# Who asks for the first eight expert blocks: ScalarE in one burst, or SP one by one between the query weights

## The chip, the cores and the metric

The kernel runs on one core of one Trainium2 chip. The metric is the device time of one execution in microseconds (us); the time of a kernel is the median of its runs.

## What is computed

Two transformer blocks on 256 tokens of width 1024. The change sits in the second half of the first block, a product-key expert layer:

```python
q = (h @ w_pq).reshape(B, S, PEER_HEADS, 2, PEER_DHALF)          # 8 heads, 2 halves of 128
sc = jnp.einsum("bshcd,hcnd->bshcn", q, sub_keys)                # 128 keys for each half
s_top, i_top = lax.top_k(sc, PEER_TOPK)                          # 16 of each half
cand = s_top[..., 0, :, None] + s_top[..., 1, None, :]
best, pos = lax.top_k(cand, PEER_TOPK)                           # 16 experts per head
gate = jax.nn.softmax(best, axis=-1)
a = jax.nn.gelu(jnp.einsum("ced,cd->ce", u_emb[idx], hx), approximate=False)
out = jnp.einsum("ce,ced->cd", g * a, v_emb[idx])                # 16384 experts in u_emb, v_emb
```

All else (convolution and window attention before it, a second block of attention and feed-forward layers behind it) is the same in both kernels.

## The kernel before, in words

All dense weights lie in one array `wst` of 279 tiles of 128x1024 floats (512 KB), used in order. `load_tile` (L140) asks for a tile on SP's queue into one of four buffers `raw`; `split_tile` makes `whi` of it on ScalarE (L150) and the rest `wlo` on VectorE (L157) or, for the tiles listed in `POOL`, in four pieces on GpSimd (L155), with three buffers of each. `mm_t` (L168) multiplies a 128x128 block three times on TensorE: `whi` with the upper half of the activations (L176), `whi` with the lower (L177), `wlo` with the upper (L178).

The **query stage** is the loop at L968 in `peer`: 16 chunks, one for each head and half, which use the tiles 66 to 81. Here a chunk goes by its number 0 to 15. Each is 24 products (L176 to L178); ScalarE copies its result to `pq` (L972), and two chunks later `scores` (L954) multiplies `pq` with the keys (L957) and ScalarE scales that to `sc` (L959). VectorE finds the 16 largest of each row (`top16`, L869 to L878) and GpSimd widens their indices (`tops`, L896). `wlo` is made by GpSimd for all chunks but 4 and 10, for these by VectorE. Work that belongs to no chunk is put in by `pump`: at chunk 3 `normalise` (L945), eight VectorE operations that write `hn` (L947). They need `rb`, the scale of each token, which comes down a chain over four engines at the head of the stage: sums of squares on TensorE (L319), their inverse root on VectorE (L363 to L369, `rr`), two diagonals `dg` on ScalarE (L380), one product on TensorE (L382), a copy on ScalarE (L383).

At the head of the stage GpSimd's queue also stores the residual, 1 MB (`park`, L847).

Behind the query stage comes the **U sweep**: 128 blocks of 128 experts, each a 512 KB tile of `ut` and eight products (`ublock`, L1050, products at L1054). The first eight blocks lie in the eight buffers `row` (`first`, L865), which lie where tensors of the stage before lay; the others go through ten buffers that were `raw`, `whi` and `wlo` (`whole`, L1038). The sweep is dense for 160 tokens. For the other 96 the rows of the chosen experts are gathered by GpSimd's queue into the same buffers `row` (L1648), which starts once the indices are known: `pick` (product L1638 on TensorE, then L1640 to L1644 on VectorE). The **V sweep** (L1168 to L1190) does the same with `vv`. From the U sweep on the order on each engine is that of the code (`in_order`).

In the query stage a scheduler sets the order on each engine from the order of the code and its own estimates, so an edit at one place can move instructions on other engines. Each engine then takes its instructions strictly in turn, and a wait holds back all that stands behind it; an engine that asks for a DMA spends its turn on it. Of the semaphores in the rows below, `DMAHW0` to `DMAHW7` count transfers asked for by SP and ScalarE, taken in turn, `DMASW` those of GpSimd, and the rest are named for the engine waited for.

Of the kernel before, what the change touches and what calls it, by code (L numbers as in the profile page):

```python
# [93 lines left out]
N = ROWS[-1][0]  # L94

RB = 8


class Kernel:
# [742 lines left out]
    def peer(self):  # L842
        nc, a = self.nc, self.a
# [19 lines left out]

        pr = self.open("rows", side="right")
        first = [pr.tile([128, D], F32, name="row", bufs=RB) for _ in range(RB)]  # L865
        for i, raw in enumerate(first):
            nc.scalar.dma_start(raw, a["ut"][i])

        def top16(v, idx, src, work):  # L869
            nc.vector.max(v[:, :8], src)  # L870
# [74 lines left out]
        def normalise():  # L945
            for cc in range(C):
                nc.vector.scalar_tensor_tensor(hn[:, cc], x[:, cc], self.p("norm2_g", cc), rb, op0=ALU.mult, op1=ALU.mult)  # L947
                yield 0.4
# [5 lines left out]
        def scores(h, c, qt):  # L954
            for tt in (1, 0):
                sp = self.pp.tile([128, 128], F32, name="ax", bufs=4)
                nc.tensor.matmul(sp, qt[:, tt * 128:(tt + 1) * 128], sk[:, 2 * h + c], start=True, stop=True)  # L957
                sc = p2t.tile([128, 128], F32, name="sc", bufs=32)
                nc.scalar.activation(sc, sp, AF.Copy, scale=r[:, tt:tt + 1])  # L959
                scs[tt, h, c] = sc  # L960

            if c == 1:
                u0, u1 = (unit(tt, h, [scs[tt, h, i] for i in range(2)]) for tt in range(2))
                firsts.append(u1)
                self.bg.insert(next((k for k, u in enumerate(self.bg) if k and u not in firsts), len(self.bg)), u1)
                self.bg.append(u0)

        for h in range(8):  # L968
            for c in range(2):
                pt = self.chunk(xs)  # L970
                qt = p2q.tile([128, T], F32, name="pq", bufs=4)
                nc.scalar.activation(qt, pt, AF.Copy)  # L972
                self.later(2, lambda h=h, c=c, qt=qt: scores(h, c, qt))
                if h * 2 + c == 3:
                    self.bg.insert(0, normalise())
                self.pump(QP, True)
        self.flush()

# [59 lines left out]
        def whole(src, n, eng=nc.sync):  # L1038

            name = ring[n % len(ring)]  # L1040
            raw = self.sp.tile([128, 1024], F32, name=name, bufs=ring.count(name))
            eng.dma_start(raw, src)
            return raw
# [6 lines left out]
        def ublock(i, n_t):  # L1050
            raw = first[i] if i < RB else whole(a["ut"][i], i - RB)
            pt = self.pp.tile([128, N], F32, name="mm", bufs=4)
            for k in range(C):
                nc.tensor.matmul(pt, raw[:, k * 128:(k + 1) * 128], hn[:, k, :N], start=(k == 0), stop=(k == C - 1))  # L1054
            self.tick()
            if n_t == 0:
                nc.scalar.activation(G(i), pt, AF.Gelu)
            else:
                ac = pg.tile([128, N], F32, name="ac", bufs=3)
                nc.scalar.activation(ac[:, :n_t], pt[:, :n_t], AF.Gelu)  # L1060
                if n_t < N:
                    nc.scalar.activation(G(i, slice(n_t, N)), pt[:, n_t:], AF.Gelu)
                muls.append((G(i, slice(0, n_t)), ac[:, :n_t]))
# [50 lines left out]
        i = 0  # L1114
# [49 lines left out]
        for q in range(4):  # L1164
            for k in range(4):
                nc.tensor.matmul(acc[q].rearrange("p a b -> p (a b)")[:, k * 128:(k + 1) * 128], zero, zero, start=True, stop=False, skip_group_check=True)
        nv = 128 - RB
        for i in range(64, 128):  # L1168
# [433 lines left out]
class RowGroup:  # L1602
# [19 lines left out]
    def activations(self):  # L1622

        nc, k = self.k.nc, self.k
        x = self.pool.tile([128, D], F32, name="row", bufs=RB)
        nc.scalar.activation(x.rearrange("p (c k t) -> p c k t", c=C, t=self.n),
# [19 lines left out]
    def row(self, table, s):  # L1646
        t = self.pool.tile([128, D], F32, name="row", bufs=RB)
        self.k.nc.gpsimd.indirect_dma_start(t, None, table, bass.IndirectOffsetOnAxis(ap=self.idx[:, s:s + 1], axis=0))  # L1648
        return t
# [20 lines left out]
def fetched(groups):  # L1670
# [4 lines left out]
    begun = []  # L1675
    for g, f, s in todo + [(None, 0, 0)] * (RB - 1):
        if g is not None:
# [193 lines left out]
```

## Time and profile before

| | us |
|---|---|
| runs | 1575.03, 1572.44, 1576.2 |
| median | 1575.03 |
| profiled execution | 1572.59 |
| its span, first to last instruction | 1570.7 |
| TensorE busy in the span | 1520.5 (97%) |
| VectorE busy | 1111.3 (71%) |
| ScalarE busy | 647.5 (41%) |
| GpSimd busy | 546.5 (35%) |

The span lies 1.9 us below the profiled execution's own time, and that 2.4 us below the median of the runs. PE stands for TensorE, PEld for its weight loads, DVE for VectorE, ACT for ScalarE, POOL for GpSimd, SP for SyncE; a q behind a name means its sequencer, which issues DMAs. TensorE is busy nearly all the time, so what can be won lies in the few stretches where it is not, or where its granted clock is below 1.

### The profile page before, as it was taken

What the parts mean: (1) busy time and instruction counts of PE and PEld (TensorE: products, weight loads), DVE (VectorE), ACT (ScalarE), POOL (GpSimd) and SP (SyncE); (2) the same over time, 40 slices, a digit from 0 to 9 for tenths busy, and PEclk for the clock granted to TensorE, in tenths of its full rate; (3) what the DMA queues carried; (4) which work ended last, traced back from release to release, by engine and by line L of the source; (5) the groups of instructions that cost most, each with busy time, mean ns of one, the idle gap of its engine ahead of it and who ended that gap; (6) DMA issues with size and microseconds to landing.
All of it is one profiled execution on the core that took longest, in us unless ns stands there. A gap on an engine that the chain in (4) does not pass through costs nothing.

```text
span 1570.7 us, 30113 instructions
## 1 busy us (share of the span) xinstructions
PE 1520.5 (97%) x11514; PEld 1462.8 (93%) x11514; DVE 1111.3 (71%) x2510; ACT 647.5 (41%) x1398; POOL 546.5 (35%) x593
## 2 busy tenths in 40 slices
PE   9999988999999998999899999999999999999997
PEld 8988987999999998999899999889999997899986
DVE  6989876979998998544344449777776558776655
ACT  4588454422355542000000034565544446655543
POOL 4957804704587776655455301000000030000000
PEclk9999999999999999999999999999999999999999
DMA  6534547449999999999999955626656586365563
GB/s 201 172 116 128 169 144 277 149 160 366 409 408 408 408 408 405 396 409 409 410 409 408 408 181 184 215 94 197 193 183 187 180 204 190 124 196 177 177 191 115
DMA packets 109680, 399.18 MB, mean 254 GB/s; under 512 B 12516, under 2 KB 12931, under 8 KB 109024
## 3 DMA queue, kind: packets, MB, share of 16 engines
q1 hardware_dynamic: 72720, 262.18, 48.2%
q0 software_dynamic: 35232, 130.64, 21.8%
q10 hardware_dynamic: 1584, 4.45, 0.8%
q8 instruction: 90, 1.47, 0.4%
q14 instruction: 54, 0.44, 0.1%
HBM read 395.04 MB, written 6.11 MB: 255 GB/s over the span
## 4 chain that ended last, share of the span: by engine, by line
PE 81%; DMA 10%; DVE 4%; issue 2%; POOL 1%; ACT 1%; ACTq 0%; POOLq 0%; DVEq 0%
PE mm L1054 17%; PE mm L176 14%; PE mm L178 13%; PE mm L177 13%; PE ax L1162 12%; DMA row<-vv,idx 3%; DMA whi<-vv 2%; DMA raw<-wst 2%; PE mm L244 2%; PE mm L243 2%; PE mm L242 2%; POOL wlo L155 1%; PE ax L1092 1%; DMA wlo<-vv 1%; DVE wlo L157 1%
## 5 line engine op out<-in xcount | busy, mean ns | idle before, releaser
L150 ACT ACTIVATE whi<-raw 128x1024 fp32r<-128x1024 f32 x275 | 290.5, 1059 | 604.4 <-PE ax L1162 281.9
L157 DVE TENSOR_TENSOR wlo<-raw,whi 128x1024 fp32r<-128x1024 f32 x213 | 262.5, 1235 | 115.0 <-ACT whi L150 110.9
L178 PE MATMUL mm<-xgh,wlo 128*128 128x256 f32 x1064 | 302.5, 284 | 3.7 <-DVE wlo L157 3.7
L176 PE MATMUL mm<-xgh,whi 128*128 128x256 f32 x1064 | 305.6, 287 | 0.0
L177 PE MATMUL mm<-xgl,whi 128*128 128x256 f32 x1064 | 302.1, 284 | 0.0
L1663 DVE SCALAR_TENSOR_TENSOR acc<-row,w,acc 128x1024 f32<-128x1024 f32 x94 | 120.8, 1285 | 153.1 <-DMA row<-vv,idx 152.8
L178 PEld LDWEIGHTS mm<-xgh,wlo 128*128 128x128 f32 x1064 | 204.9, 193 | 4.3 <-DVE wlo L157 3.9
L155 POOL TENSOR_TENSOR wlo<-raw,whi 128x256 fp32r<-128x256 f32 x248 | 180.4, 762 | 80.7 <-ACT whi L150 80.4
L176 PEld LDWEIGHTS mm<-xgh,whi 128*128 128x128 f32 x1064 | 204.8, 193 | 2.2 <-issue 1.5
L177 PEld LDWEIGHTS mm<-xgl,whi 128*128 128x128 f32 x1064 | 204.9, 193 | 0.2
L1648 POOL DMA_INDIRECT row<-vv,idx x96 | 127.0, 1323 | 99.7 <-DMA row<-vv,idx 71.0
L1162 PE MATMUL ax<-G,raw 128*128 128x160 f32 x816 | 122.2, 303 | 7.1 <-DMA raw<-vv 7.1
L1648 POOL DMA_INDIRECT row<-un,idx x96 | 110.6, 1153 | 38.6 <-DVE a L1653 18.3
L1162 PEld LDWEIGHTS ax<-G,raw 128*128 128x128 f32 x816 | 115.4, 193 | 7.4 <-DMA raw<-vv 7.4
L1653 DVE CUSTOM_DVE_ANT_0 junk<-row,h 128x1024 f32<-128x1024 f32 x96 | 120.0, 1250 | 0.4
L1054 PE MATMUL mm<-hn,raw 128*128 128x160 f32 x768 | 112.6, 300 | 0.0
L1054 PEld LDWEIGHTS mm<-hn,raw 128*128 128x128 f32 x768 | 106.3, 190 | 0.0
L177 PE MATMUL mm<-hl,whi 128*128 128x256 f32 x368 | 104.3, 283 | 0.0
L1162 PE MATMUL ax<-G,whi 128*128 128x160 f32 x624 | 95.9, 304 | 6.8 <-DMA whi<-vv 6.7
L630 DVE SCALAR_TENSOR_TENSOR ax<-u,cw,ax 128x256 f32<-128x256 f32 x227 | 99.3, 483 | 1.6 <-ACT ax L628 0.8
L1162 PEld LDWEIGHTS ax<-G,whi 128*128 128x128 f32 x624 | 89.6, 194 | 7.5 <-DMA whi<-vv 7.5
L1162 PE MATMUL ax<-G,wlo 128*128 128x160 f32 x608 | 90.8, 301 | 2.5 <-DMA wlo<-vv 2.5
(437 smaller groups left out, 3302.7 us busy)
## 6 DMA issues: line engine op xcount, KB each, us to landing
raw<-wst SPq DMA_DIRECT2D x278, 512.0 KB, 3.7
raw<-ut SPq DMA_DIRECT2D x48, 512.0 KB, 15.7
raw<-vv SPq DMA_DIRECT2D x38, 512.0 KB, 7.9
whi<-ut SPq DMA_DIRECT2D x36, 512.0 KB, 16.0
wlo<-ut SPq DMA_DIRECT2D x36, 512.0 KB, 15.7
whi<-vv SPq DMA_DIRECT2D x33, 512.0 KB, 7.8
wlo<-vv SPq DMA_DIRECT2D x26, 512.0 KB, 7.9
raw<-vv POOLq DMA_DIRECT2D x13, 512.0 KB, 17.0
```

The lines of the kernel that those rows point to most:

```text
L150: nc.scalar.activation(hi, raw, AF.Copy)
L155: nc.gpsimd.tensor_sub(lo[:, p], raw[:, p], hi[:, p])
L157: self.pin = nc.vector.tensor_sub(lo, raw, hi)
L176: nc.tensor.matmul(pt, w[:, s], xs[0][:, k], start=first, stop=False)
L177: nc.tensor.matmul(pt, w[:, s], xs[1][:, k], start=False, stop=False)
L178: nc.tensor.matmul(pt, lo[:, s], xs[0][:, k], start=False, stop=last)
L630: nc.vector.scalar_tensor_tensor(y[:, c] if k == 30 else ps, u[:, c, k:k + T], cw[:, c, k:k + 1], ps, op0=ALU.mult, op1=ALU.add)
L1054: nc.tensor.matmul(pt, raw[:, k * 128:(k + 1) * 128], hn[:, k, :N], start=(k == 0), stop=(k == C - 1))
L1162: nc.tensor.matmul(acc[d // 2][:, d % 2, :N], raw[:, d * 128:(d + 1) * 128], G(i), start=False, stop=False, skip_group_check=True)
L1648: self.k.nc.gpsimd.indirect_dma_start(t, None, table, bass.IndirectOffsetOnAxis(ap=self.idx[:, s:s + 1], axis=0))
L1653: self.k.nc.vector.tensor_tensor_reduce(junk, row, self.h, 1.0, 0.0, ALU.mult, ALU.add, self.a[:, s:s + 1])
L1663: self.k.nc.vector.scalar_tensor_tensor(self.acc, row, w, self.acc, op0=ALU.mult, op1=ALU.add)
```

## The change

The eight loads of `first` leave the head of the stage, where ScalarE asked for all of them (L866, L867), and are asked for by SP inside the loop: block k in the pass of chunk k + 3, so those of blocks 0 to 7 stand in the passes of chunks 3 to 10.

```diff
 RB = 8
+FB = 3
...
         first = [pr.tile([128, D], F32, name="row", bufs=RB) for _ in range(RB)]
-        for i, raw in enumerate(first):
-            nc.scalar.dma_start(raw, a["ut"][i])
...
                 if h * 2 + c == 3:
                     self.bg.insert(0, normalise())
+
+                if 0 <= h * 2 + c - FB < RB:
+                    nc.sync.dma_start(first[h * 2 + c - FB], a["ut"][h * 2 + c - FB])
                 self.pump(QP, True)
```

Behind the edit the line numbers of the changed kernel are higher by 1 (up to L865), lower by 1 (to L974) or higher by 2.

On SP's queue, around the query stage, `raw<-wst` are the weight tiles, `row<-ut` the eight expert blocks. Before, 81 weight tiles stood in a row ahead of the U sweep:

```order
L142 DMA raw<-wst 128x1024 x81
L1042 DMA raw<-ut 128x1024
L1042 DMA whi<-ut 128x1024
L1042 DMA wlo<-ut 128x1024
L1042 DMA raw<-ut 128x1024
```

and now, with what each waits for, from the weights of chunk 5 (first row) to those of chunk 10:

```order
L143 DMA raw<-wst 128x1024 [waits DMAHW1_49,Activation_49,Pool_49]
L977 DMA row<-ut 128x1024 [waits DMASW3_49,DMASW2_49,DMASW4_49,DMASW1_49,DVE_49]
L977 DMA row<-ut 128x1024
L977 DMA row<-ut 128x1024 [waits DMAHW2_49]
L143 DMA raw<-wst 128x1024 [waits DMAHW3_49,Activation_49,Pool_49]
L977 DMA row<-ut 128x1024 [waits DMAHW4_49]
L143 DMA raw<-wst 128x1024 [waits DMAHW5_49,Activation_49,Pool_49]
L977 DMA row<-ut 128x1024 [waits DMAHW6_49]
L143 DMA raw<-wst 128x1024 [waits DMAHW7_49,DVE_49]
L977 DMA row<-ut 128x1024 [waits DMAHW0_49]
L143 DMA raw<-wst 128x1024 [waits DMAHW1_49,Activation_49,Pool_49]
```

Three blocks now stand between the weights of chunks 5 and 6, then one behind the weights of each of the chunks 6 to 10.

On ScalarE at the head of the query stage, before:

```order
L867 DMA row<-ut 128x1024 [waits PE_49]
L867 DMA row<-ut 128x1024 x3
L867 DMA row<-ut 128x1024 [waits DMAHW3_49]
L867 DMA row<-ut 128x1024 [waits DMAHW4_49]
L867 DMA row<-ut 128x1024 [waits DMAHW5_49]
L867 DMA row<-ut 128x1024 [waits DMAHW6_49]
L972 ACTIVATE pq<-mm 128x256 [waits PE_49]
L380 ACTIVATE dg<-ident,rr 128x128 [waits DVE_49]
L380 ACTIVATE dg<-ident,rr 128x128
L972 ACTIVATE pq<-mm 128x256 [waits PE_49] x2
L150 ACTIVATE whi<-raw 128x1024 [waits Pool_49]
L383 ACTIVATE rb<-ax 128x256 [waits PE_49]
```

and now (`c_4400` and `c_4409` are two small tables for the gathered rows, which came later before):

```order
L1621 DMA c_4400<-cst 128x194
L1621 DMA c_4409<-cst 128x164
L151 ACTIVATE whi<-raw 128x1024
L971 ACTIVATE pq<-mm 128x256
L381 ACTIVATE dg<-ident,rr 128x128 x2
L971 ACTIVATE pq<-mm 128x256
L151 ACTIVATE whi<-raw 128x1024
L384 ACTIVATE rb<-ax 128x256
```

The eight loads are gone from ScalarE, and `whi` of chunk 3 stands ahead of the first `pq`. On TensorE the product with `dg` (L382, now L383) moved ahead by 19 products: it stood behind the last product of chunk 2 and stands now behind the fifth.

On VectorE at chunk 4, before:

```order
L947 SCALAR_TENSOR_TENSOR hn<-x,prm,rb 128x256 [waits Activation_49]
L947 SCALAR_TENSOR_TENSOR hn<-x,prm,rb 128x256 x7
L157 TENSOR_TENSOR wlo<-raw,whi 128x1024 [waits DMAHW4_49,PE_49,Activation_49]
L870 MAX tv<-sc 128x8 [waits Activation_49]
L872 MAX_INDEX iu<-tv,sc 128x8 [waits DVE_49]
```

and now:

```order
L158 TENSOR_TENSOR wlo<-raw,whi 128x1024 [waits DMAHW4_49,PE_49,Activation_49]
L946 SCALAR_TENSOR_TENSOR hn<-x,prm,rb 128x256 [waits Activation_49]
L946 SCALAR_TENSOR_TENSOR hn<-x,prm,rb 128x256 x7
L869 MAX tv<-sc 128x8 [waits Activation_49]
L871 MAX_INDEX iu<-tv,sc 128x8 [waits DVE_49]
```

`wlo` of chunk 4 now stands ahead of the eight `hn`. On GpSimd the first `tops` (L896, now L895), which needs the first `top16`, moved from behind `wlo` of chunk 6 to ahead of it.

## Rows read from the trace of the kernel before

**Rows 1.** The head of the page.

```profile
span 1570.7 us, 30113 instructions
```

**Rows 2.** Windows: stretch, its length, PE, PEld, DVE, ACT, POOL busy, PE clock, DMA share, GB/s.

```profile
260.00:265.00 5.00, 1.12 (x10) 0.91 (x8) 0.00 (x0) 0.35 (x2) 0.00 (x0) 1.00 1.01 414
265.00:270.00 5.00, 4.33 (x18) 3.73 (x19) 2.59 (x4) 4.79 (x11) 2.82 (x4) 0.66 1.03 419
270.00:275.00 5.00, 2.27 (x20) 2.06 (x18) 5.00 (x6) 1.85 (x4) 5.00 (x7) 1.00 0.62 214
275.00:280.00 5.00, 4.00 (x21) 4.00 (x22) 4.83 (x25) 0.00 (x0) 3.74 (x5) 0.66 0.78 233
```

**Rows 3.** The chain that ended last, in order of time: start, length, what.

```profile
253.58 10.07 DMA raw<-wst
...
268.11 6.17 DVE hn L947 x7
```

**Rows 4.** TensorE's timeline: start, length, line, operation [idle before <-releaser].

```profile
260.84 0.28 PE L178 MATMUL mm<-xgh,wlo 128*128 128x256 f32 x1
265.66 0.70 PE L382 MATMUL ax<-dg,ones 128*128 128x256 f32 x2 [4.54 <-ACT dg L380]
266.20 0.99 PE L957 MATMUL ax<-sk,pq 128*128 128x128 f32 x4
...
276.00 0.38 PE L178 MATMUL mm<-xgh,wlo 128*128 128x256 f32 x1 [3.73 <-DVE wlo L157]
...
280.24 0.61 PE L957 MATMUL ax<-sk,pq 128*128 128x128 f32 x4
...
283.51 0.61 PE L957 MATMUL ax<-sk,pq 128*128 128x128 f32 x4
```

**Rows 5.** ScalarE's timeline, and line L867 by itself (duration in ns: min/median/max).

```profile
252.63 0.34 ACTq L867 DMA_DIRECT2D row<-ut  x1
...
253.59 11.02 ACTq L867 DMA_DIRECT2D row<-ut  x6
264.65 0.38 ACT L972 ACTIVATE pq<-mm 128x256 f32<-128x256 f32 x1 [11.13 <-DMA raw<-wst]
...
L867 ACTq DMA_DIRECT2D row<-ut x8: 335/551/997, 252.6 to 264.1; - x8
```

**Rows 6.** Timelines of VectorE and GpSimd.

```profile
257.80 0.16 DVE L369 SCALAR_TENSOR_TENSOR rr<-ax,rr 128x2 f32<-128x2 f32 x1
267.41 6.88 DVE L947 SCALAR_TENSOR_TENSOR hn<-x,prm,rb 128x256 f32<-128x256 f32 x8 [9.45 <-ACT rb L383]
274.21 1.74 DVE L157 TENSOR_TENSOR wlo<-raw,whi 128x1024 fp32r<-128x1024 f32 x1
...
277.44 0.28 DVE L878 FIND_INDEX8 iu<-tv,scw 128x8 uint32<-128x128 f32 x1
...
254.07 2.80 POOL L155 TENSOR_TENSOR wlo<-raw,whi 128x256 fp32r<-128x256 f32 x4
```

**Rows 7.** An SP issue, DMA issues (KB, median us to landing), two windows as in rows 2.

```profile
256.90 0.33 SPq L142 DMA_DIRECT2D raw<-wst  x1
...
raw<-wst SPq DMA_DIRECT2D x278, 512.0 KB, 3.7
...
254.00:260.00 6.00, 6.00 (x54) 6.00 (x53) 2.33 (x12) 0.00 (x0) 2.85 (x5) 1.00 0.87 291
260.00:270.00 10.00, 5.44 (x28) 4.64 (x27) 2.59 (x4) 5.14 (x11) 2.82 (x4) 0.83 1.02 416
```

**Rows 8.** A wait within 245 to 320 us (total, times, longest); gathers; the pick; a window.

```profile
DVE tv L870 <- ACT sc L959: 3.0, 2, 1.7
...
L1648 POOL DMA_INDIRECT row<-un,idx x96: 943/976/1909, 357.3 to 614.9; - x96
...
352.53 0.29 DVE L1640 TENSOR_TENSOR own<-ax,c 128x128 f32<-128x128 f32 x1 [7.10 <-PE ax L1638]
...
360.00:900.00 540.00, 523.59 (x3984) 520.61 (x3983) 367.17 (x678) 111.09 (x410) 325.42 (x270) 0.99 1.02 406
```

## The prediction
> **What bounds the kernel now.** I read the page first, then windows over the query stage, then the chain of waits through the hole that they show, and last the timeline of each engine in it. The span is 1570.7 us [rows 1]. The query stage runs from about 252 to 318 us, and TensorE works through it without a break except in one place: of the 5 us from 260 it works 1.12, of those from 270 it works 2.27, and in the two slices between and behind them its granted clock is 0.66, a mixture of its two levels, 2.4 and 1.2 GHz, where it had been 1.00 [rows 2]. Each drop of the clock follows an idle stretch. The chain of waits leads through the same hole: a weight load that took 10.07 us and, behind ScalarE's late turn, seven of VectorE's `hn` [rows 3].
>
> How much does the hole cost? In the undisturbed part one chunk with its pair of score products takes 283.51 - 280.24 = 3.27 us, of which the scores are about 0.44 and the 24 products 2.83 [rows 4]. Between the last product of chunk 2, whose issue slot ends at 260.84 + 0.12 = 260.96, and the scores at 280.24 TensorE did the product with `dg` (266.20 - 265.66 = 0.54) and two such chunks (3, 4) with their scores: 0.54 + 2 x 3.27 = 7.08 us of work in 19.28 us. **The hole costs 12.2 us.** Its pieces: 4.7 idle up to 265.66, waiting for `dg` from ScalarE; 3.9 idle up to 276.00, waiting for `wlo` of chunk 4 from VectorE [rows 4]; the other 3.6 are the work done at the lower clock behind each.
>
> Why was ScalarE late? It asks for the first block at 252.63 and is then held in its own queue: the last six issues lie in one stretch of 11.02 us, and the copy `pq` behind them waited 11.13 us, in the end for a weight load [rows 5]. In the order, the fifth to eighth loads each wait on a DMA semaphore that a weight load of SP uses. So ScalarE stood still until a weight load had landed that itself had 2 MB of blocks and the 1 MB of `park` for company: 10.07 us [rows 3] where such a load normally takes 3.7 [rows 7]. Why was VectorE late? `rb` came late out of ScalarE, the eight `hn` took 6.88 us, and `wlo` of chunk 4 stood behind them [rows 6].
>
> **The change part by part.** *ScalarE loses eight issues and four waits.* By its new order it makes `whi` of chunk 3 as soon as chunk 0 has left its buffer (about 254.4 to 255.5), copies `pq` (255.9), and waits for `rr`, which VectorE ends at 257.96 [rows 6]; two `dg` follow by about 258.7. TensorE reaches the product with `dg` after five products of chunk 2, at about 258.05 + 5 x 0.12 = 258.65. With the passing on of the semaphore I charge a **new wait of 0.2 us**. The two small loads `c`, now ahead of `whi`, take less than the 0.9 us which ScalarE has before chunk 0 ends. From there TensorE finds every operand ready: chunk 2 ends at 261.6 with the `dg` product, scores and chunk 3 at 264.9, scores and chunk 4 at 268.2, the third scores at 268.6, where before they ended at 280.7. **The stage ends 12.2 - 0.2 = 12.0 us sooner.**
>
> *VectorE does `wlo` of chunk 4 ahead of `hn`.* `whi` of chunk 4 comes at about 260.2, `wlo` at 261.5 to 262.0 (1.23 us, or 1.74 as in rows 6), and TensorE wants it at 265.4. This move is needed: with `rb` at 260.5 and `hn` first, `wlo` would come at 260.5 + 6.88 + 1.74 = 269.1, and 3.7 us of idle time would stay.
>
> *What hides `hn` now.* VectorE ends it at 262.0 + 6.88 = 268.9 at the latest. The first `top16` ended 277.72 - 275.95 = 1.8 us behind the `wlo` [rows 6], so it ends by 270.7; GpSimd's first `tops` (0.4) waits for it, and `wlo` of chunk 6 stands behind that `tops`: its first quarter (2.80 / 4 = 0.7 [rows 6]) is there by 271.8. TensorE starts chunk 6 at 268.6 + 3.27 = 271.9 and needs `wlo` 0.2 later. **This is the tightest margin, 0.3 us**; I take no cost, and 0 to 2 us as its bounds, 2 if `hn` starts that much later.
>
> *SP gains eight issues, and the weights behind them wait in its queue.* An issue takes 0.33 us of SP [rows 7], which has nothing else to do. Ahead of the weights of chunk 6, asked for at 256.90 [rows 7], now lie `park` (1.05 MB), the weights of chunk 5 (0.52) and three blocks (1.57); with their own 0.52 that is 3.67 MB from 254 on. At the measured rates, 291 GB/s up to 260 and 416 after it [rows 7], they land at 260 + (3.67 - 1.75) / 0.416 = 264.6; at 291 throughout, at 266.6. TensorE's start at 271.9 needs them 1.9 us earlier (1.06 `whi`, 0.7 for a quarter of `wlo`), at 270.0. The cost lies between 0 (3.4 us to spare) and, should they take much longer, what the rival below has; I take 0. Each further chunk brings 1.05 MB in 3.27 us, 321 GB/s, under the 416 shown.
>
> The Trainium skill (page DMA: Bandwidth & Descriptors, section Queues, rings and completion order) says that each DMA engine takes the descriptors of one ring in their order, and that it goes round between the rings of different queues packet by packet. This rule speaks against the change, since a weight load in SP's ring now has the blocks in front of it and not beside it; the sum above already takes it so. The trace of before shows the other arrangement not helping much, a weight load in a ring of its own taking 10.07 us [rows 3].
>
> *Is it kept to the end?* Behind the stage TensorE is nearly full (523.59 of 540 us) and DMA saturated (406 GB/s) [rows 8], so a shift survives only if the gathers start earlier too. They start at 357.3, behind the pick, whose indices VectorE had 7.1 us before TensorE reached the product that it needs [rows 8]. VectorE reaches its `top16` at about 268.9 for 275.95, 7.1 us sooner, and before, it idled 3.0 us more waiting for later scores [rows 8], idle time that it does not have now. So VectorE moves by about 10 against TensorE's 12, and 7.1 us of slack covers the rest. The bytes in the saturated stretch are the same. I count the whole 12.0 as kept.
>
> **The sum.** 1572.59 - 12.0 = 1560.6 for an execution like the profiled one, and 1575.0 - 12.0 = **1563.0 us** for the median, which lies 2.4 above it. What a measurement can tell from no change is about 0.2%, 3.2 us.
>
> **The rivals.**
> - *Part of the hole comes back* (GpSimd behind `tops`, or weights later than 270): 2 us idle, and about as much again at the lower clock, as the 8.6 idle us cost 3.6 more before; with both, 4 to 6 us. Time 1567 to 1569. For it: the margin of 0.3. Against it: the 6.88 was measured beside a busy GpSimd, which is idle for part of the new stretch. Chance 0.14.
> - *Only the issuing is saved.* Eight issues of 0.551 us [rows 5] are 4.4 us: 1570.6. This holds if the slow weight load and not ScalarE's turn makes the hole, since the bytes stay the same. Against it: the idle 4.7 us ended with ScalarE's `dg` and not with a weight [rows 4], and nothing but its own queue kept ScalarE from that. Chance 0.07. The Trainium skill (the same page, section Issuing engines are not separate DMA queues) states the rule behind this: all issuers share the same 16 DMA engines, and spreading issues saves only sequencer time, usually small. The trace does not agree with "small" here: 11.02 us, because waits sat between the issues.
> - *The gain drowns in the saturated sweeps*: 1575, no change. Against it: the start of the gathers hangs on TensorE's order and not on a time. Chance 0.05.
> - *Slower: SP is held at the first block.* That load waits for VectorE and four counts of GpSimd's DMAs until its buffer is free, and behind it on SP stand the weights of every later chunk, which had nothing in front of them before. Held until T, SP delivers the weights of chunk 6 at about T + 3 + 2.1 / 0.416 = T + 8, wanted at 270. With some 2 us at the lower clock all 12 us are gone at T = 272; held until 278, the time is 1581. Against it: ScalarE got the same buffers at 252.63 without a wait [rows 5]. Chance 0.03.
>
> **How the numbers follow.** The forecast has 0.71, with a range of its own of 1560.5 to 1565.5 (0.2 to 2 us of new waits, 1.5 for the spread of the medians). The range that holds 8 in 10 takes in the first rival: 1559.5 to 1570. Faster by over 0.2%: 0.71 + 0.14 + 0.07 = 0.92; within it 0.05; slower 0.03.
>
> **What would show it right or wrong.** In the changed profile no stretch of issuing on ScalarE like that of L867; the product with `dg` at about 259 and not 265.7; the third pair of scores ending at about 268.6; a granted clock of 1.00 in every slice from 255 to 285; the first gather at about 345. Wrong would be an idle TensorE behind GpSimd's `wlo` of chunk 6 or behind a weight load, a first block asked for by SP much later than 254, or gathers that start at 357 though the stage ended sooner.

## The result and the profile after

| | before | after |
|---|---|---|
| runs | 5, 1572.44 to 1578.92 us | 5, 1565.32 to 1566.38 us |
| median | 1576.2 us | 1566.05 us |
| profiled execution | 1572.59 us | 1565.32 us |
| its span | 1570.7 us | 1562.1 us |

The ratio is 0.9942, with an interval of 0.9928 to 0.9956: faster, by 7 to 11 us. Two later comparisons gave 1564.27 against 1575.87 us (0.9926, 0.9913 to 0.9940) and 1563.97 against 1577.29 us (0.9911, 0.9898 to 0.9925). The three gains are 10.2, 11.6 and 13.3 us; the forecast was 12.0 and 1563.0 us, with a range of 1559.5 to 1570.

In the profile after, the head of the query stage (the first product of L319, now L320) lies at 256.85 us in place of 254.41, though nothing ahead of it was changed. The 2.4 us arise at the very start: the program's first product on L382 (now L383) stands at 18.95 us before and at 21.37 after. So 2.44 us are added to a time of before when the two are compared. The windows of the stage, columns as in [rows 2], and last the sweeps, as in [rows 8]:

```profile
255.00:260.00 5.00, 5.00 (x46) 5.00 (x46) 2.58 (x13) 2.29 (x5) 4.98 (x9) 1.00 0.83 178
260.00:265.00 5.00, 5.00 (x42) 4.88 (x41) 2.99 (x7) 3.00 (x6) 2.10 (x4) 1.00 1.01 415
265.00:270.00 5.00, 5.00 (x45) 5.00 (x44) 4.70 (x13) 1.53 (x5) 3.63 (x5) 1.00 1.03 418
270.00:275.00 5.00, 5.00 (x45) 5.00 (x44) 3.91 (x22) 3.57 (x9) 4.62 (x8) 1.00 1.03 411
275.00:280.00 5.00, 5.00 (x45) 5.00 (x45) 4.93 (x31) 3.31 (x8) 5.00 (x9) 1.00 1.02 402
360.00:900.00 540.00, 522.82 (x3976) 518.57 (x3975) 362.55 (x636) 108.72 (x402) 319.23 (x262) 0.99 1.02 406
```

The hole is gone: TensorE works all of every slice and its granted clock stays at 1.00, where [rows 2] had 1.12 and 2.27 busy us of 5 and a clock of 0.66. The sweeps look as before (522.82 busy us of 540, 406 GB/s).

TensorE's timeline of the kernel after, which answers to [rows 4]:

```profile
256.85 0.50 PE L320 MATMUL ax<-ones,sq 128*128 128x1 f32 x4
...
261.19 0.70 PE L383 MATMUL ax<-dg,ones 128*128 128x256 f32 x2
...
270.51 0.61 PE L956 MATMUL ax<-sk,pq 128*128 128x128 f32 x4
```

Neither the product with `dg` nor the third scores has a wait in front of it. In the frame of before they stand at 258.75 and 268.07 us, where they had stood at 265.66 and 280.24. ScalarE, against [rows 5]:

```profile
255.07 0.33 ACTq L1621 DMA_DIRECT2D c<-cst  x1
...
260.44 0.69 ACT L381 ACTIVATE dg<-ident,rr 128x128 f32<-128x128 f32 x2 [2.13 <-DVE rr L370]
...
264.18 1.06 ACT L151 ACTIVATE whi<-raw 128x1024 fp32r<-128x1024 f32 x1 [1.56 <-PE mm L179]
...
269.50 1.06 ACT L151 ACTIVATE whi<-raw 128x1024 fp32r<-128x1024 f32 x1 [3.47 <-DMA raw<-wst]
```

The stretch of 11.02 us is gone: `dg` follows `rr` at once. The last row is `whi` of chunk 6, which waited for its weights; TensorE did not notice. VectorE and GpSimd, against [rows 6]:

```profile
262.39 1.23 DVE L158 TENSOR_TENSOR wlo<-raw,whi 128x1024 fp32r<-128x1024 f32 x1 [1.98 <-ACT whi L151]
263.53 4.69 DVE L946 SCALAR_TENSOR_TENSOR hn<-x,prm,rb 128x256 f32<-128x256 f32 x8
...
265.32 3.50 POOL L156 TENSOR_TENSOR wlo<-raw,whi 128x256 fp32r<-128x256 f32 x4 [3.22 <-ACT whi L151]
269.87 0.40 POOL L895 CAST tops<-iu 128x256 f16<-128x256 uint32 x1 [1.05 <-DVE iu L877]
270.64 2.82 POOL L156 TENSOR_TENSOR wlo<-raw,whi 128x256 fp32r<-128x256 f32 x4 [0.38 <-ACT whi L151]
```

`wlo` of chunk 4 is out of the way before `hn`, and `hn` took 4.69 us in place of 6.88, with GpSimd idle for 1.8 us of it. SP's issues, against [rows 7]:

```profile
256.53 2.54 SPq L977 DMA_DIRECT2D row<-ut  x3
259.34 0.54 SPq L143 DMA_DIRECT2D raw<-wst  x1
259.93 0.60 SPq L977 DMA_DIRECT2D row<-ut  x1
262.13 0.33 SPq L143 DMA_DIRECT2D raw<-wst  x1
```

SP was not held at the first block. Its first three issues took 2.54 us, 1.69 of them the third, where an issue without a wait takes 0.33: one wait of about 1.4 us. The weights of chunk 6 were asked for at 259.34 and landed 10.1 us later (KB and us to landing; then the windows around them):

```profile
raw<-wst SPq DMA_DIRECT2D x1, 512.0 KB, 10.1
...
256.44:262.44 6.00, 6.00 (x52) 5.88 (x51) 2.39 (x13) 3.33 (x7) 5.64 (x9) 1.00 1.00 287
262.44:269.50 7.06, 7.06 (x63) 7.06 (x62) 6.96 (x16) 2.03 (x6) 3.50 (x4) 1.00 1.01 413
```

And the pick with the gathers, against [rows 8] (there a wait of 7.10 us and a first gather at 357.3):

```profile
342.81 0.29 DVE L1642 TENSOR_TENSOR own<-ax,c 128x128 f32<-128x128 f32 x1 [6.60 <-PE ax L1640]
...
L1650 POOL DMA_INDIRECT row<-un,idx x96: 941/976/1909, 347.6 to 605.2; - x96
```

### The profile page after: what moved, and what is told of

It reads as the page before. It is cut to its first block, busy times and chain, and to the rows that moved or that the text cites. A ratio compares the mean times of both kernels' runs of the same rounds, so it can differ in the third digit from the quotient of the medians.

```text
span 1562.1 us, 30116 instructions
## 1 busy us (share of the span) xinstructions
PE 1519.1 (97%) x11514; PEld 1461.0 (94%) x11514; DVE 1107.7 (71%) x2510; ACT 647.4 (41%) x1398; POOL 543.5 (35%) x593
## 4 chain that ended last, share of the span: by engine, by line
PE 80%; DMA 13%; DVE 4%; issue 2%; ACT 1%; POOL 1%; POOLq 0%; DVEq 0%; ACTq 0%
PE mm L1056 18%; PE mm L177 14%; PE mm L179 14%; PE mm L178 14%; PE ax L1164 7%; DMA wlo<-vv 6%; DMA raw<-vv 3%; DMA whi<-vv 2%; PE mm L245 2%; PE mm L244 2%; PE mm L243 2%; PE ax L1094 1%; DVE wlo L158 1%; PE mm L175 1%; DMA raw<-wst 1%
## 5 line engine op out<-in xcount | busy, mean ns | idle before, releaser
L1164 PEld LDWEIGHTS ax<-G,raw 128*128 128x128 f32 x816 | 115.0, 193 | 10.2 <-DMA raw<-vv 10.1
```

The costliest lines, as they stand in the source:

```text
L1164: nc.tensor.matmul(acc[d // 2][:, d % 2, :N], raw[:, d * 128:(d + 1) * 128], G(i), start=False, stop=False, skip_group_check=True)
```

## Where the time went

One count serves for all runs. The stage is taken from the first product of L319 to the first product of the U sweep; the sweeps from there to the start of the V sweep's last group of products; the rest to the end of the span.

| kernel | head | stage | sweeps | gathers start behind the U sweep's start | U sweep's start to end of span | median, ratio |
|---|---|---|---|---|---|---|
| before | 254.4 | 63.4 | 611.7 | 39.5 | 1252.9 | 1576.2 |
| before_again | 255.8 | 62.3 | 611.7 | 39.6 | 1253.7 | |
| after | 256.9 | 51.2 | 612.4 | 39.5 | 1254.0 | 1566.05, 0.9942 |
| again | 256.5 | 51.0 | 613.5 | 39.6 | 1254.7 | 1564.27, 0.9926 |
| after_beside | 255.8 | 50.6 | 613.7 | 39.5 | 1255.6 | 1563.97, 0.9911 |
| sp_burst | 254.9 | 56.4 | 612.4 | 39.5 | 1253.2 | 1568.64, 0.9958 |
| act_spread | 255.5 | 49.8 | 613.4 | 39.8 | 1255.6 | 1562.7, 0.9918 |
| act_spread_2 | 256.2 | 49.8 | 611.5 | 39.7 | 1253.9 | 1565.12, 0.9921 |
| act_tiny | 256.5 | 52.8 | 613.9 | 39.5 | 1256.7 | 1566.63, 0.9941 |
| act_four | 255.7 | 57.5 | 612.0 | 39.6 | 1253.8 | 1571.34, 0.9962 |
| hn_first | 258.0 | 52.2 | 611.5 | 39.6 | 1254.3 | 1565.66, 0.9930 |
| pick_early | 255.6 | 50.7 | 612.1 | 33.2 | 1254.8 | 1563.03, 0.9913 |
| pick_late | 255.5 | 50.8 | 621.7 | 53.2 | 1262.7 | 1571.11, 0.9960 |

The stage became 63.4 - 51.2 = 12.2 us shorter. The span became only 8.6 us shorter, since in that one execution the head lay 2.4 us later and the part behind the stage was 1.1 us longer: 12.2 - 2.4 - 1.1 = 8.7. Among all runs, none of which changes anything ahead of the stage, the head lies from 254.4 to 258.0, and the last part takes 1252.9 to 1256.7 without pick_late. In the last part, though, the three runs that ask for all eight whole blocks in one row (before, before_again, sp_burst) are the three shortest, 1252.9 to 1253.7 against 1253.8 to 1256.7. That the change costs nothing there, some 1.5 us on average, is therefore not shown.

## The experiments

Theory of the prediction: ScalarE's turn, held by waits between its own DMA issues, and VectorE's order, `hn` ahead of `wlo`, made the hole. Rivals: the burst of 4.2 MB itself, whoever asks for it; the engine that asks; and, for the end of the program, that the gathers' start decides how much is kept.

**Both kernels once more, unchanged** (before_again, again, after_beside).

> The kernel before, one more profile. If the place of the head of the query stage is a matter of the execution, it lies anywhere from 254 to 258 us here (254.4 in the first profile, 256.9 in that of the changed kernel), and the stretch from the head to the U sweep is 63.4 +- 0.5. If the 2.4 us come from the change, the head lies at 254.4 again.

> The changed kernel once more, for the size of the gain and for how far two executions of the same program differ before the query stage. From the first of the sums of squares at the head of the query stage (L319/L320) to the first product of the U sweep the kernel before took 254.4 to 317.8 = 63.4 us and the changed one 256.9 to 308.1 = 51.2. If the 2.4 us by which the changed profile was late at the head of the stage belong to the execution and not to the change, this stretch is again 51.2 +- 0.3 while the head lies anywhere from 254 to 257.5, and the time is 9 to 12 us below before. If the change itself makes the stage start late, the head lies at 256.9 again.

> The changed kernel once more, on the chip of the next three, as their measure. Both theories: 1564 to 1567 us, 50.9 to 51.5 us from the first product of L320 to the first product of the U sweep.

Stages of 62.3, 51.0 and 50.6 us: a gain of 11.3 to 11.7 here. In these three a chunk took 3.18 us (the scores at 285.81 and 288.99 in again), in the first two profiles 3.27. Over 16 chunks that makes 1.4 us, but the stage of the changed kernel was only 0.2 and 0.6 us shorter: at the quicker pace TensorE came to wait near the end of the stage for GpSimd's `wlo`, which it did not at 3.27. First again, then after_beside:

```profile
303.21 0.38 PE L179 MATMUL mm<-xgh,wlo 128*128 128x256 f32 x1 [0.49 <-POOL wlo L156]
...
302.12 0.39 PE L179 MATMUL mm<-xgh,wlo 128*128 128x256 f32 x1 [0.27 <-POOL wlo L156]
```

So stages are compared below only at equal pace: before, after, sp_burst and act_four at 3.27, the others at 3.18.

**sp_burst: SP asks, but for all eight in a row** (the kernel before, edited).

```diff
-            nc.scalar.dma_start(raw, a["ut"][i])
+            nc.sync.dma_start(raw, a["ut"][i])
```

> All eight blocks asked for by SP at the head of the stage, in one go. If ScalarE's held turn made the hole (my theory), the product with dg comes as early as in the changed kernel and chunks 3 to 5 run without a break; but the weights of chunk 6 lie behind 4.2 MB of blocks in one queue and land some 3 us later than wanted, so 3 us idle and 1 to 3 us at the lower clock: 55 to 57 us from the head to the U sweep, 4 to 6 us slower than the changed kernel, still 6 us faster than before. If the burst itself makes the hole (4 MB of blocks and park in front of the weights, whoever asks), the stretch is 60 to 64 us, as before. If only ScalarE matters and the spreading nothing, 51.2.

A stage of 56.4 us. SP's, ScalarE's and TensorE's timelines and a window:

```profile
254.61 9.77 SPq L867 DMA_DIRECT2D row<-ut  x8
...
273.87 1.06 ACT L150 ACTIVATE whi<-raw 128x1024 fp32r<-128x1024 f32 x1 [4.37 <-DMA raw<-wst]
...
274.97 0.39 PE L176 MATMUL mm<-xgh,whi 128*128 128x256 f32 x1 [2.85 <-ACT whi L150]
...
275.00:280.00 5.00, 4.62 (x23) 4.22 (x24) 3.23 (x17) 2.79 (x5) 5.00 (x8) 0.70 0.33 116
```

The early hole is gone, a new one stands 9 us later: now SP's turn is held, 9.77 us, and the weights of chunk 6 come behind it and all eight blocks. The clock falls behind the new idle stretch as it did before. So 7.0 of the 12.2 us (63.4 - 56.4) come with ScalarE free and `wlo` of chunk 4 ahead of `hn`, as this kernel has it too, and the spreading brings the rest. The medians say the same: 1568.64 lies between 1575.87 and 1564.27, the two kernels beside it.

**act_spread, act_spread_2: spread as in the change, but ScalarE asks** (the kernel after, edited).

```diff
-                    nc.sync.dma_start(first[h * 2 + c - FB], a["ut"][h * 2 + c - FB])
+                    nc.scalar.dma_start(first[h * 2 + c - FB], a["ut"][h * 2 + c - FB])
```

> ScalarE asks, but for one block in each pass as the changed kernel does. My theory: the waits in ScalarE's queue are then on transfers that landed long ago, and an issue costs 0.55 us of an engine that is busy 60% of the stage: 51.2 to 52.5 us from the head to the U sweep, within 2 us of the changed kernel. If what counts is that ScalarE issues at all, the stretch is 4 us longer (55 or more).

> The same edit as act_spread, once more beside the changed kernel. If it does not matter which engine asks as long as the blocks are spread, the two medians lie within 1.5 us of each other, and the 49.8 us of the first run was its pace of 3.18 us a chunk. If ScalarE's own queue is better for the blocks than SP's, since the weights then have no block in front of them in theirs, this one is 1.5 us or more faster again.

A stage of 49.8 us both times and no wait of TensorE in it. ScalarE's timeline, one issue of eight alike:

```profile
260.80 0.35 ACTq L977 DMA_DIRECT2D row<-ut  x1
```

Against the kernel after the medians were 1562.7 to 1564.27 and, beside it, 1565.12 to 1563.97: not to be told apart. Which engine asks makes no difference that the medians show; that it asks when nothing has to be waited for does. The stage is 0.8 us shorter than in after_beside at the same pace, and without the wait for GpSimd near its end. The Trainium skill (page DMA: Bandwidth & Descriptors, section Issuing engines are not separate DMA queues) says that all issuers share the same 16 DMA engines; this pair does not speak against it.

**act_tiny: ScalarE's held turn without the bytes.** The kernel after, and at the head ScalarE asks besides for the first 64 columns of each block, 32 KB; SP later loads the whole blocks over them.

```diff
+        for i, raw in enumerate(first):
+            nc.scalar.dma_start(raw[:, :64], a["ut"][i][:, :64])
```

> The changed kernel, and in addition ScalarE asks at the head of the stage for 32 KB of each of the eight blocks (1/16 of it), so its eight turns and its waits are back but not the bytes; VectorE's order falls back to hn ahead of wlo of chunk 4. My theory: ScalarE is held only until the weights of chunk 5 have landed at their normal 4 to 5 us, some 5 us instead of 11, then hn stands ahead of wlo: 2 to 5 us idle and 1 to 2 at the lower clock, 55 to 58 us from the head to the U sweep. If the burst of bytes made the hole and not the turns, 51.2 to 52. If the issuing alone, 4 us.

A stage of 52.8 us, less loss than expected. ScalarE's and TensorE's timelines:

```profile
255.53 5.61 ACTq L868 DMA_DIRECT2D row<-ut  x6
...
262.20 0.70 PE L383 MATMUL ax<-dg,ones 128*128 128x256 f32 x2 [1.05 <-ACT dg L381]
...
269.87 0.39 PE L179 MATMUL mm<-xgh,wlo 128*128 128x256 f32 x1 [1.15 <-DVE wlo L158]
```

The turn is held again, but for 5.61 us and not 11.02. That the same waits hold it, and end sooner because the weight load had no 2 MB beside it, is the likely reading; the profile names no transfer here, and the small loads themselves can have been part of it. `dg` is then 1.05 us late for TensorE, and the clock stayed at 1.00. So the hold by itself is real, and its price was much lower without the burst. SP had to wait for the small loads too (three issues in 5.62 us), so the run is not a clean measure of ScalarE alone.

**hn_first: the kernel after with VectorE's old order**, `wlo` of chunk 4 (tile 70) held behind the last `hn`.

```diff
-            self.pin = nc.vector.tensor_sub(lo, raw, hi)
+            with self.tc.issue_after(self.tail.ins) if self.wt == 70 else nullcontext():
+                self.pin = nc.vector.tensor_sub(lo, raw, hi)
```

> The changed kernel with one order undone: wlo of chunk 4 stands behind the eight hn on VectorE again; all else in order as changed but for one place on SP (blocks 4 and 5 trade places with a weight tile). If that order was needed (my theory), TensorE waits for wlo of chunk 4: rb is there at 262.6 in the changed profile, hn takes 4.7 to 6.9 us, wlo 1.2 to 1.7, so wlo comes at 268.5 to 271.2 and TensorE wants it at 267.7: 1 to 3.5 us idle and 0 to 2 at the lower clock, 52 to 57 us from the head to the U sweep instead of 51.2. If the order on VectorE is of no matter, 51.2 +- 0.3.

VectorE, GpSimd and TensorE:

```profile
263.77 3.74 DVE L947 SCALAR_TENSOR_TENSOR hn<-x,prm,rb 128x256 f32<-128x256 f32 x8 [2.25 <-ACT rb L385]
267.43 1.75 DVE L159 TENSOR_TENSOR wlo<-raw,whi 128x1024 fp32r<-128x1024 f32 x1
...
266.37 4.10 POOL L156 TENSOR_TENSOR wlo<-raw,whi 128x256 fp32r<-128x256 f32 x4 [3.15 <-ACT whi L151]
...
269.24 0.38 PE L180 MATMUL mm<-xgh,wlo 128*128 128x256 f32 x1 [0.20 <-DVE wlo L159]
```

TensorE waited 0.20 us and not 3.7: `hn` took 3.74 us, about half of the 6.88, with GpSimd idle beside most of it. The stage of 52.2 us lies in the range expected, but for another reason: of the 1.2 to 1.6 us more than in again and after_beside, this wait is 0.20, while two waits for GpSimd's `wlo` near the end are 0.26 and 0.51; the rest is not broken down.

**act_four: half of the burst without a hold.** ScalarE asks for four blocks at the head, none of which waits for a transfer, SP for the other four later (the kernel after, edited).

```diff
+        for i, raw in enumerate(first[:4]):
+            nc.scalar.dma_start(raw, a["ut"][i])
...
-                if 0 <= h * 2 + c - FB < RB:
+                if 4 <= h * 2 + c - FB < RB:
```

> ScalarE asks for four blocks at the head, none of which waits for a transfer, and SP for the other four later. Theory of the held queue: ScalarE is through with its issues in 1.4 us, the product with dg comes about 5 us behind the head as in the changed kernel, and the stage takes 51 to 53 us whatever the weight load beside the blocks takes. Rival, the burst: 2.1 MB beside the weights in a queue of their own make a weight load take 8 to 10 us as before, TensorE waits 2 to 5 us for whi of chunk 3 or 4 though dg is in time, its clock falls, and the stage takes 55 to 59 us.

A stage of 57.5 us, 6.3 more than in the kernel after at the same pace, as the rival had it, but not by its mechanism. TensorE, VectorE, GpSimd, and two windows:

```profile
263.84 0.38 PE L177 MATMUL mm<-xgh,whi 128*128 128x256 f32 x1 [0.32 <-ACT whi L151]
...
272.73 0.39 PE L179 MATMUL mm<-xgh,wlo 128*128 128x256 f32 x1 [3.22 <-DVE wlo L158]
...
264.09 6.92 DVE L948 SCALAR_TENSOR_TENSOR hn<-x,prm,rb 128x256 f32<-128x256 f32 x8 [4.83 <-ACT rb L384]
270.94 1.74 DVE L158 TENSOR_TENSOR wlo<-raw,whi 128x1024 fp32r<-128x1024 f32 x1
...
263.86 10.79 POOL L156 TENSOR_TENSOR wlo<-raw,whi 128x256 fp32r<-128x256 f32 x12 [5.69 <-ACT whi L151]
...
270.00:275.00 5.00, 2.27 (x14) 2.27 (x15) 5.00 (x20) 0.80 (x1) 4.86 (x6) 0.88 1.03 405
275.00:280.00 5.00, 5.00 (x36) 5.00 (x36) 2.55 (x18) 2.17 (x3) 2.66 (x6) 0.78 0.61 226
```

No wait of TensorE or ScalarE ended here with a late weight load, and the product with `dg` had none in front. In this kernel's order, though, more than the loads is as it was before: the product with `dg` stands behind all of chunk 2, so `hn` starts 8.4 us behind the head (5.8 in hn_first); `hn` stands ahead of `wlo`; and GpSimd makes the `wlo` of three chunks in a row beside it, so `hn` takes 6.92 us. Together these give back the second of the two stretches of the hole without any hold: 3.22 us idle here, 3.73 in [rows 4], and a lower clock behind it. `hn` ahead of `wlo` alone does not, as hn_first shows (0.20). Both theories of this run missed it; the prediction's step on `hn` had named the order as a cause.

**pick_early and pick_late: the gathers earlier and later.** The number is how many background steps the U sweep takes in per block until the gathers are asked for; it moves the pick and what goes with it, not the stage.

```diff
-UP = (1.5, 1.3)
+UP = (2.0, 1.3)
```

```diff
-UP = (1.5, 1.3)
+UP = (1.0, 1.3)
```

> The changed kernel with the background work spread more densely over the first U blocks (budget 2.0 instead of 1.5 for a block), so that the pick stands behind 11 blocks instead of 14. VectorE had the indices 6.6 us before TensorE reached the pick in the changed profile. If the DMA-saturated sweeps are what carries a shift to the end (my theory: they end when their bytes are through, and start with the gathers), the first gather comes 5 to 6.6 us earlier and the time falls by 3 to 6 us, to 1560 to 1563. If TensorE's own work bounds the sweeps, the gathers come earlier and the time stays within 1.5 us of the changed kernel.

> The tasks of the U sweep are put in more slowly (1.0 in place of 1.5 per block until the gathers are asked for), so that the gathers start later behind the U sweep's start, by some 5 to 10 us against the changed kernel's 39.5. If the gathers' start sets the end of the two sweeps, the time from the U sweep's first to the V sweep's last product grows by as much, to 617 to 622 us. If the sweeps are bound by TensorE and the bytes and the gathers have slack, it stays at 611 to 614 us and the time at that of the changed kernel.

Gathers that start 6.4 us earlier (33.18 us behind the U sweep's start for 39.55) leave the sweeps at 612.1 us, so the theory of pick_early, that the sweeps end sooner with them, was wrong. Gathers that start 13.6 us later (53.18) make them 621.7, 8.0 more than beside them in after_beside. The end of the V sweep shows why. VectorE's last `acc`, which adds up the gathered rows, and TensorE's products L1669 that take it, first in after_beside:

```profile
896.92 1.28 DVE L1665 SCALAR_TENSOR_TENSOR acc<-row,w,acc 128x1024 f32<-128x1024 f32 x1 [3.77 <-DMA row<-vv,idx]
...
905.89 0.53 PE L1669 MATMUL ax<-c,acc 128*128 128x64 f32 x4
```

and in pick_late:

```profile
909.07 2.60 DVE L1665 SCALAR_TENSOR_TENSOR acc<-row,w,acc 128x1024 f32<-128x1024 f32 x2 [0.53 <-DMA row<-vv,idx]
...
905.62 0.33 PE L1669 MATMUL ax<-c,acc 128*128 128x64 f32 x2
911.73 0.63 PE L1669 MATMUL ax<-c,acc 128*128 128x32 f32 x2 [5.78 <-DVE acc L1665]
...
912.00:915.00 3.00, 3.00 (x13) 3.00 (x14) 0.81 (x1) 0.00 (x0) 0.00 (x0) 0.50 0.40 89
915.00:918.00 3.00, 3.00 (x21) 3.00 (x21) 1.55 (x4) 1.52 (x4) 0.00 (x0) 0.79 0.21 86
```

In after_beside the gathered half is ready at 896.92 + 1.28 = 898.20, 7.7 us before TensorE wants it; in pick_late TensorE stands still for 5.78 us, and 13.6 - 7.7 = 5.9. The other 2.2 of the 8.0 us are the lower clock behind it, 0.50 and 0.79 in the two windows (3 x 0.50 + 3 x 0.21 = 2.1). In the first profiles the margin was 4.1 us before and 4.7 after, so it is some 4 to 8 us. Earlier gathers only widen it: it is 12.5 us in pick_early.

## Why the prediction was right, and where it was not

**What made the hole: right, with the parts interlocked.** The forecast took 12.2 us off the stage less 0.2; 12.2 went in the two profiles at the same pace, 11.3 and 11.7 in the repeats. The product with `dg` was foreseen for 258.65, it stood at 258.75; the third scores were to end at about 268.6, they did at 270.51 + 0.45 - 2.44 = 268.5. The new wait of 0.2 us did not occur. Of the two stretches, the first needs both the waits between ScalarE's issues and the burst beside them: it is 1.05 idle us in place of 4.54 without the bytes (act_tiny), and none where SP makes the burst or ScalarE half of it without a wait (sp_burst, act_four). The second came with `hn` ahead of `wlo` only where `rb` was late and GpSimd busy besides (3.22 in act_four); with `rb` in time and GpSimd idle beside most of `hn` it was 0.20 (hn_first). Which of these two weighs more no run here separates.

**VectorE's order: the length of `hn` mis-sized.** The 3.7 us that the old order was said to leave were 0.20 in hn_first, the run that undoes this order and little else. The step used one length of `hn`, 6.88 us, for every place. It is 3.25 to 6.9 us, the longer the more GpSimd works beside it; with 3.74 the step's own sum leaves 0.6 us. With `rb` in time, little of the 12 us hung on this move.

**The tightest margin: mis-sized for the same reason.** With `hn` at 4.69 us, `tops` came at 269.87, GpSimd then waited for `whi` and not for VectorE, and the first quarter of `wlo` of chunk 6 at 270.64 + 0.7 = 271.3; TensorE wanted it at about 271.9 + 2.4 = 274.3. The margin was 3 us and not 0.3. The first rival had its 0.14 from it.

**The weights of chunk 6: later than said, without a price.** They were to land at 264.6, or 266.6 by the lower rate; `whi` started on them at 269.50 - 2.44 = 267.06. The rates were not to blame: in the stretch that answers to the 254 to 260 of the step, 256.44 to 262.44, the transfers moved at 287 GB/s, and at 413 behind it, near the 291 and 416 assumed. At these rates some 4.6 MB had moved when the weights landed, where the step had 3.67, their own included. So some 0.9 MB were transfers that the step did not count: up to 0.18 the two small tables, the rest perhaps those that SP asked for later (a block at 259.93, a weight tile at 262.13). The rows do not separate them. Still 2.9 us were left of the 5.4 foreseen. sp_burst shows the price beyond that margin: 2.85 us idle and a clock of 0.70.

**Issued by SP: as said.** The first block was asked for at 256.53, three issues took 2.54 us with one wait of about 1.4, and nothing behind came too late: the slower rival did not come. That only the issuing is saved (4.4 us) fell too: the same 4.2 MB moved in the same stage, 12.2 us shorter.

**Kept to the end: right, by a looser tie.** "A shift survives only if the gathers start earlier too" needs a margin in it. The gathers did start 357.3 - 347.6 = 9.7 us earlier in the profile, 12.1 in the frame of the head (foreseen: about 345; 345.2). Had they not moved at all against the 9.7, a margin of 4 to 8 us would have taken most of it, and 2 to 6 us would have been lost; this case was not run by itself, only a delay of 13.6 us in pick_late. Whether the last part of the program gave back 1 to 2 us of the gain stays open, as said above.

**The sum.** The profiled execution was to take 1560.6 and took 1565.32 us, 4.7 us more: 2.4 by the later head, 1.1 by the longer last part, and 1.3 because its time lies 3.2 us above its span and not 1.9. The step from one profile to a sum has no room for any of them. The three medians, 1566.05, 1564.27 and 1563.97, lie around 1564.8 on average, 1.8 above the forecast. The first, from the comparison that the prediction was about, lies 0.55 above the forecast's own range up to 1565.5, in the wider one up to 1570; the other two lie inside both.

## What to carry to other kernels

A compute engine that asks for DMAs can pay far more for the waits between the issues than for the issues, here 11.02 us for six in place of 0.33 to 0.55 for one: look whether the order shows a DMA semaphore inside a row of issues, and space the issues so that each finds it free, on whichever queue. When such a hold is removed, go through what stood behind it on the other engines in their new order, since the same edit can keep or give back the second half of the gain. Where a stage's gain must pass through a later stage, find the place where a side path joins and read its margin there.

## What was not expected of the hardware

**VectorE and GpSimd slow each other.** The eight `hn` took 3.25 us with GpSimd idle (act_spread_2), 3.74, 4.69, 6.88 and 6.92 us, the more the longer GpSimd's `wlo` ran beside them, and GpSimd's four pieces 2.82, 3.50 and 4.10 us; VectorE's own `wlo` 1.23 or 1.75. The Trainium skill (page SBUF — State Buffer, section SBUF: two separate sides) says that a VectorE operation with two SBUF inputs and a GpSimd operation that reads SBUF take turns on one shared pair of ports, the later one blocked for the whole instruction. That both sides lengthen agrees with it; that it is a turn and not a slower pace, these rows don't show. In act_spread_2, where GpSimd was idle, VectorE and GpSimd:

```profile
262.81 3.25 DVE L946 SCALAR_TENSOR_TENSOR hn<-x,prm,rb 128x256 f32<-128x256 f32 x8
...
267.88 2.83 POOL L156 TENSOR_TENSOR wlo<-raw,whi 128x256 fp32r<-128x256 f32 x4 [6.48 <-ACT whi L151]
```

**One chunk took 3.27 us in some executions and 3.18 in others, all at a granted clock of 1.00**, the same kernel among them (after 3.27, again 3.18). What differs stays open. It is worth up to 1.4 us over the stage, less where another engine then becomes the slower one, and a comparison of two profiles should look for it first.
